# Splitting the feed-forward input inside the output projection, and multiplying by the row factor afterwards

## The chip, the cores and the metric

The kernel runs on one core of a Trainium2 chip. The metric is the device time of one execution in microseconds; the time of a kernel is the median of its runs. The engines are named as in the profile: PE (TensorE matmul), DVE (VectorE), ACT (ScalarE), POOL (GpSimd) and SP (SyncE, which issues the DMAs).

## What is computed

The reference is one inference step of a two-layer decoder trunk for a prompt of 1024 tokens and 8 sample tokens, 1032 rows in all, D_MODEL 1024, D_FF 3072. Each layer is a mixer and a convolved feed-forward block. What the change touches is the end of the mixer and the first half of the feed-forward:

```python
def _rmsnorm(x, g):
    r = lax.rsqrt(jnp.mean(x32 * x32, axis=-1, keepdims=True) + EPS)
    return (x32 * r * g).astype(x.dtype)

def _conv_ffn(x, buf, w_up, cw, cb, w_down):
    u = x @ w_up
    u, nbuf = _causal_dwconv(u, buf, cw, cb)      # three taps along the tokens
    return (jax.nn.gelu(u[..., :D_FF]) * u[..., D_FF:]) @ w_down, nbuf

# in _trunk, for each layer l
x = x + jnp.concatenate([main, mo], axis=-1) @ prm['w_out'][l]
hn = _rmsnorm(x, prm['norm_ffn_g'][l])
f, fc = _conv_ffn(hn, ffn_conv0[l], ...)
x = x + f
```

For the 8 samples the two earlier tokens of the convolution come from a state and not from the sequence. The factor r is one number for each token, the gain g one for each channel.

## The kernel before

**Layout.** Activations lie with the channels on the 128 partitions and the tokens along the row: 8 channel tiles of 1032 tokens. The tokens are cut into two halves of 516 (`HALF`) and four quarters of 258 (`QW`). A float32 operand is carried as a pair of reduced floats, hi (a rounded copy, made on ACT by `acopy`, L105) and lo (the operand less hi, made on DVE by `vtt`, L113, or on POOL by `gtt`, L116); each product is three matmuls (`mm3`, L298 to L300: hi by hi, hi by lo, lo by hi).

**Output projection** (`out_proj`, L775). For each half `hb` and each output tile `m`, two quarters of 24 matmuls of 258 columns, 48 matmuls a tile, 384 a half. `get` loads the weights one tile ahead and splits them (hi of 128x1024 on ACT, lo on POOL). The residual row of a tile comes by DMA when the tile is first met (`residual`, L768; in layer 0 from `x_t`, in layer 1 from a spill), DVE adds the finished sum to it, and `on_tile` (L1320) stores the new quarter to `rD` (L1322) and adds its square to a running sum over the tiles.

**Entry of the feed-forward** (`enter_ffn`, L1309). After the last tile of a half, `inverse` sums the squares over the channels with a matmul by ones (L1334) for both quarters and makes r of them; `norm` then scales every tile by g and r (DVE, L119) and makes the operands of the up projection. That projection is a seven-product scheme after Strassen and Winograd: per pair `j` of an up gate tile and an up value tile (24 pairs), products P1 to P7 of 4 x 3 matmuls on each half, 168 matmuls a pair. Its left operands are sums of quarters of the weights, made by `combine` (L832; 11 POOL operations of 128x512, of which 7 are lo parts, and 7 ACT copies a pair), its right operands B11, B21, B22, T1 to T4 sums of quarters of the normed residual, made by `norm`. The weights of pair 0 are made by `first_pair`, which is spawned when the first half of the projection is done; what is spawned advances a step at each `tick`.

**Up stage** (`ffn`, L858). The list `SEQUENCE` runs pair 0 one half at a time, then pairs 1 to 23 whole; weights are combined five products ahead (`AHEAD`). DVE adds the products from PSUM into two rows `ug` and `uv` of 1032. When a pair is done, `post` convolves: ACT makes the centre tap of 1032 columns and the bias (`act_conv`), DVE adds two shifted taps for each row (L119, 128x1023 and 128x1022) and the sample columns' state (128x8), ACT takes the gelu, DVE multiplies gate and value (128x1032), and SP stores the result to `gD`. POOL copies the last 10 columns of each row into `ul`.

**Order.** A scheduler places the instructions of DVE, POOL, PE and SP; ACT keeps the order of the program in layer 0 and in the feed-forward of both layers. Rows come from a pool of 44 buffers, small tiles from a pool of 12.

## Time and profile before

| | us |
|---|---|
| median of 3 runs | 2542.76 |
| range of the runs | 2539.66 to 2547.52 |
| the profiled execution | 2545.75 |
| its span | 2544.0 |
| PE busy in the span | 2339.4 (92%) |
| DVE, ACT, POOL busy | 1582.0, 1075.7, 1419.4 |
| mean granted TensorE clock | 0.961 |

The span is what the trace covers; 1.75 us of the profiled execution lie around it. A busy time is the sum of an engine's instructions. Granted clock 1.00 is 2.4 GHz and 0.50 is 1.2 GHz. In the timeline a number in brackets is the idle time ahead of an instruction and what ended it.

### The profile page before, as it was taken

How to read it: one execution, taken by the hardware profiler on the slowest of the kernel's cores; microseconds unless marked ns; L12 is line 12 of the kernel's file. 1: busy time of each engine (PE TensorE's matmuls, PEld its weight loads, DVE VectorE, ACT ScalarE, POOL GpSimd, SP SyncE). 2: the span in 40 equal slices, each digit the busy share in tenths (PEclk: the TensorE clock that was granted, in tenths of full speed). 3: DMA queues.
4: the chain of work that ended last, by engine and by line, in shares of the span. 5: the costliest groups of instructions: out<-in, count | busy, mean ns of one | idle time of the engine just before them, and what ended most of it. 6: DMA issues, size and time to landing. Idle time of an engine off the chain costs nothing.

```text
span 2544.0 us, 42855 instructions
## 1 busy us (share of the span) xinstructions
PE 2339.4 (92%) x16590; PEld 2255.1 (89%) x16590; DVE 1582.0 (62%) x2850; ACT 1075.7 (42%) x2253; POOL 1419.4 (56%) x1123
## 2 busy tenths in 40 slices
PE   7996877799999999999988988787999999999999
PEld 5896867789999999999977778687999999999999
DVE  6659975666666666432477789875666666663321
ACT  5665542344444344211265576643444344442110
POOL 2147743578888886312144356335888888853220
PEclk9998978899999999999999999898999999999999
DMA  4221124212222224421575544552122222254311
GB/s 165 85 69 56 44 77 150 75 67 76 76 84 85 83 76 177 164 91 58 166 237 171 201 141 133 149 166 73 67 84 84 84 76 76 76 211 135 97 56 64
DMA packets 142491, 273.64 MB, mean 108 GB/s; under 512 B 28544, under 2 KB 85456, under 8 KB 142288
## 3 DMA queue, kind: packets, MB, share of 16 engines
q1 hardware_dynamic: 142288, 270.91, 31.7%
q8 instruction: 130, 2.13, 0.3%
q14 instruction: 73, 0.60, 0.1%
HBM read 211.99 MB, written 58.87 MB: 106 GB/s over the span
## 4 chain that ended last, share of the span: by engine, by line
PE 64%; DVE 8%; issue 2%; ACT 2%; DMA 2%; POOL 1%; SPq 0%; POOLq 0%; ACTq 0%; DVEq 0%
PE ps L299 21%; PE ps L298 21%; PE ps L300 21%; DVE row L113 2%; ACT row L105 1%; DVE sm L113 1%; DVE row L119 1%; POOL row L116 1%; DVE ty L113 1%; DVE ty L396 1%; DMA row<-in_w_out 1%; DVE ty L119 0%; DMA row<-mD 0%; ACT sm L105 0%; PE ps L422 0%
## 5 line engine op out<-in xcount | busy, mean ns | idle before, releaser
L116 POOL TENSOR_TENSOR row<-row,row 128x512 fp32r<-128x512 f32 (+9 forms) x754 | 1164.6, 1566 | 789.4 <-ACT row L105 472.8
L298 PE MATMUL ps<-row,row 128*128 128x258 f32 (+4 forms) x5032 | 1511.9, 303 | 54.5 <-ACT row L105 44.4
L299 PE MATMUL ps<-row,row 128*128 128x258 f32 (+4 forms) x5032 | 1509.5, 302 | 27.9 <-DVE row L113 18.6
L300 PE MATMUL ps<-row,row 128*128 128x258 f32 (+4 forms) x5032 | 1471.0, 301 | 20.5 <-POOL row L116 20.5
L298 PEld LDWEIGHTS ps<-row,row 128*128 128x128 f32 x5032 | 963.7, 192 | 73.1 <-ACT row L105 49.8
L299 PEld LDWEIGHTS ps<-row,row 128*128 128x128 f32 x5032 | 965.1, 192 | 43.7 <-DVE row L113 24.1
L300 PEld LDWEIGHTS ps<-row,row 128*128 128x128 f32 x5032 | 948.4, 192 | 30.9 <-POOL row L116 23.4
L105 ACT ACTIVATE row<-row 128x512 fp32r<-128x512 f32 (+8 forms) x756 | 492.8, 690 | 922.5 <-POOL row L116 303.3
L113 DVE TENSOR_TENSOR row<-row,ps 128x258 f32<-128x258 f32 (+2 forms) x736 | 322.2, 444 | 700.7 <-PE ps L300 655.0
L119 DVE SCALAR_TENSOR_TENSOR row<-row,fw,row 128x1023 f32<-128x1023 f32 x192 | 264.7, 1397 | 67.3 <-ACT row L105 67.3
L113 DVE TENSOR_TENSOR row<-row,row 128x258 fp32r<-128x258 f32 (+7 forms) x268 | 242.9, 930 | 29.8 <-ACT row L105 15.8
L105 ACT ACTIVATE row<-ps 128x258 f32<-128x258 f32 (+6 forms) x430 | 157.3, 406 | 65.4 <-PE ps L300 26.1
L116 POOL TENSOR_TENSOR row<-row,ty 128x768 f32<-128x768 f32 (+2 forms) x56 | 77.3, 1381 | 157.7 <-DVE ty L413 55.2
L105 ACT ACTIVATE row<-row,fw 128x1032 f32<-128x1032 f32 x96 | 114.8, 1244 | 59.2 <-DVE row L113 59.1
L105 ACT ACTIVATE sm<-row 128x258 f32<-128x258 f32 (+3 forms) x130 | 54.6, 452 | 192.4 <-DVE row L113 129.4
L113 DVE TENSOR_TENSOR row<-row,sb 128x8 f32<-128x8 f32 x96 | 112.3, 1169 | 0.0
L113 DVE TENSOR_TENSOR sm<-sm,sm 128x258 f32<-128x258 f32 (+5 forms) x125 | 80.8, 652 | 24.8 <-ACT sm L105 23.3
L105 ACT ACTIVATE row<-ps,ty,ty 128x256 f32<-128x256 f32 (+1 forms) x160 | 87.4, 564 | 8.3 <-DVE ty L113 8.0
L105 ACT ACTIVATE sm<-ps 128x384 f32<-128x384 f32 (+5 forms) x156 | 65.0, 445 | 38.2 <-PE ps L431 24.1
L113 DVE TENSOR_TENSOR row<-ps,row 128x384 fp32r<-128x384 f32 (+2 forms) x125 | 63.3, 518 | 19.4 <-ACT row L105 8.1
L116 POOL TENSOR_TENSOR sm<-sm,row 128x192 f32<-128x192 f32 (+3 forms) x72 | 49.2, 696 | 34.1 <-ACT sm L105 18.6
L116 POOL TENSOR_TENSOR row<-row 128x512 f32<-128x512 f32 x48 | 62.0, 1291 | 2.5 <-DVE row L119 2.5
(164 smaller groups left out, 1485.5 us busy)
## 6 DMA issues: line engine op xcount, KB each, us to landing
row<-in_w_ffn_up SPq DMA_DIRECT2D x96, 512.0 KB, 3.2
gD<-row SPq DMA_DIRECT2D x48, 516.0 KB, 2.6
row<-gD SPq DMA_DIRECT2D x48, 516.0 KB, 6.2
row<-in_w_ffn_down SPq DMA_DIRECT2D x64, 384.0 KB, 3.0
row<-hD SPq DMA_DIRECT2D x48, 512.0 KB, 6.6
row<-in_w_out SPq DMA_DIRECT2D x32, 512.0 KB, 4.1
rD<-row SPq DMA_DIRECT2D x64, 129.0 KB, 2.0
row<-rD SPq DMA_DIRECT2D x16, 516.0 KB, 8.5
```

The source lines that it names most:

```text
L105: return nc.scalar.activation(out, in_, func, **kw)
L113: return V.tensor_tensor(out=out, in0=a, in1=b, op=op)
L116: return G.tensor_tensor(out=out, in0=a, in1=b, op=op)
L119: return V.scalar_tensor_tensor(out=out, in0=a, scalar=s, in1=b, op0=op0, op1=op1)
L298: T.matmul(out, ah, bh, start=first and j == 0, stop=False, skip_group_check=more)
L299: T.matmul(out, ah, bl, start=False, stop=False, skip_group_check=more)
L300: T.matmul(out, al, bh, start=False, stop=last and j == n - 1, skip_group_check=more)
L396: V.tensor_reduce(out=mx[:, c0 : c0 + m], in_=s3, axis=AX.X, op=amax, negate=True)
```

## The change

**1. The factor.** r is no longer multiplied into the operands. They are made of x times g alone, which is linear in them, and the finished rows `ug` and `uv` of every pair are multiplied by r (128x1032 on DVE, two a pair) ahead of the convolution. r itself is made once a layer, for the four quarters together, at step 10 of `SEQUENCE`; the multiplication by ones stands there, four matmuls.

**2. The split.** `on_tile` writes x times g back over the residual (ACT), and after each second-half tile `combine_x` makes T2, T3 and T4 of its four quarters (four differences and three lo parts of 128x258 on DVE, three hi on ACT). When a half is done `settle` makes the other four operands in copies of 516 columns (ACT), with lo on DVE for the gate half and POOL for the other. The tiles run in the order 0, 4, 1, 5, 2, 6, 3, 7.

**3. The residual.** It comes in half rows, two channel tiles in a row, and one fetch ahead of its use.

**4. The weights of pair 0.** `first_pair` is spawned ahead of the projection, one half earlier.

**5. The samples.** The state is added for 12 pairs at once on POOL, with gelu and gate over 96 columns (`samples`), and stored apart. The centre tap's gate side, gelu, gate multiplication and store are 1024 columns wide; the two 128x8 additions of a pair are gone.

```diff
+    def unspill(t, hb, kk):
+        for a in range(2):
+            k, d = kk + 4 * a, t[:, a * HALF : a * HALF + HALF]
+            if hb == 0:
+                SY.dma_start(d[:, : 4 * P].rearrange("p (i t) -> p i t", i=4), xD[0:4, :, k, :].rearrange("i p t -> p i t"))
+                SY.dma_start(d[:, 4 * P : HALF], xD[4, :, k, : HALF - 4 * P])
...
+    def residual(l, hb, kk):
+        t = row()
         if l:
-            return unspill(m)
-        t = row()
-        SY.dma_start(t[:, :NT], I["x_t"][:, m, :])
+            unspill(t, hb, kk)
+        else:
+            SY.dma_start(
+                t[:, : 2 * HALF].rearrange("p (a t) -> p a t", a=2),
+                I["x_t"].rearrange("p (a k) t -> p a k t", a=2)[:, :, kk, hb * HALF : hb * HALF + HALF],
+            )
         return t
...
+        fetch()
         for hb in range(2):
-            for m in range(KD):
+            for m in TILES:
                 key = f"out{l}.{hb}.{m}"
                 wh, wl = get(key, 1, 1)
-                if x[m] is None:
-                    x[m] = residual(l, m)
+                if m < 4:
+                    fetch()
...
-                    vtt(x[m][:, c0 : c0 + QW], x[m][:, c0 : c0 + QW], p[:, :QW], add)
-                    on_tile(q, m)
+                    on_tile(hb, part, m, p[:, :QW])
                     tick()
...
         def act_conv(u, t):
+            vtt(u[:, :NT], u[:, :NT], factor()[:, :NT], mul)
             a = row()
-            act(a[:, :NT], u[:, :NT], AF.Identity, scale=fwc(2, t), bias=fbc(t))
+            act(a[:, :SEQ], u[:, :SEQ], AF.Identity, scale=fwc(2, t), bias=fbc(t))
...
-            vtt(a[:, SEQ:NT], a[:, SEQ:NT], sb3[:, :, t], add)
...
-            vtt(ag[:, :NT], ag[:, :NT], av[:, :NT], mul)
-            SY.dma_start(gD[l, j], ag[:, :NT])
+            vtt(ag[:, :SEQ], ag[:, :SEQ], av[:, :SEQ], mul)
+            SY.dma_start(gD[l, j, :, :SEQ], ag[:, :SEQ])
+            if j % SG == SG - 1:
+                samples(j - SG + 1)
...
+        def samples(j0):
+            pair = []
+            for t0 in (j0, KF + j0):
+                t = sm()[:, : 8 * SG].rearrange("p (b j) -> p b j", b=8)
+                w = fw[:, None, 2 * MU + t0 : 2 * MU + t0 + SG].to_broadcast([P, 8, SG])
+                gtt(t, ul3[:, 2:10, t0 : t0 + SG], w, mul)
+                gtt(t, t, sb3[:, :, t0 : t0 + SG], add)
+                pair.append(t)
+            act(pair[0], pair[0], AF.Gelu_apprx_tanh)
+            o = sm()[:, : 8 * SG].rearrange("p (j b) -> p j b", b=8)
+            gtt(o.rearrange("p j b -> p b j"), pair[0], pair[1], mul)
+            SY.dma_start(gD[l, j0 : j0 + SG, :, SEQ:NT].rearrange("j p b -> p j b"), o)
...
+            if q == 10:
+                factor()
...
+        def on_tile(hf, part, m, p):
+            q = 2 * hf + part
+            xs, t = place(hf, part, m), sm()
+            vtt(t[:, :QW], xs, p, add)
+            SY.dma_start(rD[l, m, :, QB[q] : QB[q] + QW], t[:, :QW])
+            acopy(xs, t[:, :QW], scale=g_ffn[l][m])
...
+            if part == 0 and wait:
+                combine_x(*wait.pop())
+            if part == 1 and m >= 4:
+                wait.append((hf, m - 4))
+
+        def combine_x(hf, kk):
...
+            vtt(t3, d, b, sub)
+            vtt(b, b, a, sub)
+            vtt(t2, d, b, sub)
+            vtt(t4, c, t2, sub)
+            for name, t in (("T3", t3), ("T2", t2), ("T4", t4)):
...
+                split(name, kk, hf, own[name][:, o : o + QW], own[name][:, o + QW : o + HALF], t)
+
+        def settle(hf):
...
+                    acopy(hi, raw)
+                    (gtt if a else vtt)(lo, raw, f(hi), sub)
...
+        gen["w"] = spawn(first_pair())
+
         def on_half(hf):
...
-            gen[hf] = start(norm(hf))
-            if not hf:
-                gen["w"] = spawn(first_pair())
+            gen[hf] = start(settle(hf))
```

Three places of the order, before and with the change. First POOL in layer 0's projection, at the tiles of the first half; `in_w_out` rows are the projection's weights, 128x1024 their lo parts. Before:

```order
L116 TENSOR_TENSOR row_699_3862<-row_692_3797,row_698_3861 128x1024
L116 TENSOR_TENSOR row_707_3930<-row_700_3865,row_706_3929 128x1024
L116 TENSOR_TENSOR row_715_3998<-row_708_3933,row_714_3997 128x1024
L116 TENSOR_TENSOR row_731_4089<-row_716_4001,row_730_4088 128x1024
L116 TENSOR_TENSOR row_647_3464<-row_669_3595,row_646_3463 128x258
L116 TENSOR_TENSOR row_651_3472<-row_685_3731,row_650_3471 128x258
```
With the change (row_664 and row_665 hold the two raw weight tiles of pair 0):

```order
L118 TENSOR_TENSOR row_672_3601<-row_659_3489,row_671_3600 128x1024
L118 TENSOR_TENSOR row_681_3673<-row_665_3530 128x512
L118 TENSOR_TENSOR row_677_3638<-row_664_3528,row_677_3638 128x512
L118 TENSOR_TENSOR row_681_3673<-row_681_3673,row_664_3528 128x512
L118 TENSOR_TENSOR row_664_3528<-row_664_3528,row_665_3530 128x512
L118 TENSOR_TENSOR row_682_3676<-row_681_3673,row_682_3676 128x512
L118 TENSOR_TENSOR row_684_3680<-row_673_3604,row_683_3679 128x1024
L118 TENSOR_TENSOR row_681_3673<-row_664_3528,row_681_3673 128x512
L118 TENSOR_TENSOR row_696_3735<-row_664_3528,row_696_3735 128x512
L118 TENSOR_TENSOR row_700_3771<-row_664_3528,row_700_3771 128x512
L118 TENSOR_TENSOR row_702_3775<-row_685_3683,row_701_3774 128x1024
```
Before, POOL has nothing but the projection's lo parts up to the norm's 128x258 pieces; with the change, the weight sums and lo parts of pair 0 (128x512) stand between them, up to five between two lo parts.

Second, SP at the start of the same projection. Before:

```order
L251 DMA row_633_3326<-in_w_out 128x1024
L1286 DMA out_1<-yl_144 128x54
L251 DMA row_658_3487<-in_w_out 128x1024
L772 DMA row_659_3489<-in_x_t 128x1032
L802 DMA row_662_3524<-in_ffn_state 128x768
L1322 DMA rD_91<-row_659_3489 128x258
L805 DMA out_9<-row_662_3524 1024x1x48
L1322 DMA rD_91<-row_659_3489 128x258
L251 DMA row_668_3593<-in_w_out 128x1024
L772 DMA row_669_3595<-in_x_t 128x1032
```
With the change:

```order
L253 DMA row_633_3326<-in_w_out 128x1024
L783 DMA row_656_3483<-in_x_t 128x2x516
L1326 DMA out_1<-yl_144 128x54
L253 DMA row_659_3489<-in_w_out 128x1024
L783 DMA row_660_3491<-in_x_t 128x2x516
L844 DMA row_664_3528<-in_w_ffn_up 128x1024
L844 DMA row_665_3530<-in_w_ffn_up 128x1024
L823 DMA row_666_3532<-in_ffn_state 128x768
L1366 DMA rD_91<-sm_662_3518 128x258
L826 DMA out_9<-row_666_3532 1024x1x48
L1366 DMA rD_91<-sm_668_3588 128x258
```
The residual's DMA stands ahead of the store of `out_1` and is followed by the next one ahead of the first `rD` store; the two loads of pair 0's weights (`in_w_ffn_up`) have come in.

Third, DVE in one pair of the steady up stage, from the last additions of a pair to its gate multiplication; `ps` are products in PSUM, `fw` holds the taps, `sb` the sample state. Before:

```order
L113 TENSOR_TENSOR row_834_5100<-row_834_5100,ps_837_5124 128x258
L113 TENSOR_TENSOR row_838_5137<-row_838_5137,ps_845_5211 128x258
L113 TENSOR_TENSOR row_838_5137<-row_838_5137,ps_846_5224 128x258
L119 SCALAR_TENSOR_TENSOR row_849_5298<-row_838_5137,fw_100,row_849_5298 128x1023
L113 TENSOR_TENSOR row_849_5298<-row_849_5298,sb_101 128x8
L119 SCALAR_TENSOR_TENSOR row_850_5304<-row_834_5100,fw_100,row_850_5304 128x1023
L113 TENSOR_TENSOR row_850_5304<-row_850_5304,sb_101 128x8
L119 SCALAR_TENSOR_TENSOR row_849_5298<-row_838_5137,fw_100,row_849_5298 128x1022
L119 SCALAR_TENSOR_TENSOR row_850_5304<-row_834_5100,fw_100,row_850_5304 128x1022
L113 TENSOR_TENSOR row_858_5372<-row_854_5336,ps_856_5346 128x258
L113 TENSOR_TENSOR row_858_5372<-row_854_5336,ps_857_5359 128x258
L113 TENSOR_TENSOR row_849_5298<-row_849_5298,row_850_5304 128x1032
```
With the change (row_861 holds the factor of the four quarters):

```order
L115 TENSOR_TENSOR row_907_5359<-row_907_5359,ps_910_5381 128x258
L115 TENSOR_TENSOR row_911_5394<-row_911_5394,ps_918_5468 128x258
L115 TENSOR_TENSOR row_907_5359<-row_907_5359,row_861_4969 128x1032
L115 TENSOR_TENSOR row_911_5394<-row_911_5394,ps_919_5481 128x258
L115 TENSOR_TENSOR row_911_5394<-row_911_5394,row_861_4969 128x1032
L121 SCALAR_TENSOR_TENSOR row_922_5556<-row_911_5394,fw_100,row_922_5556 128x1023
L121 SCALAR_TENSOR_TENSOR row_923_5562<-row_907_5359,fw_100,row_923_5562 128x1023
L121 SCALAR_TENSOR_TENSOR row_922_5556<-row_911_5394,fw_100,row_922_5556 128x1022
L121 SCALAR_TENSOR_TENSOR row_923_5562<-row_907_5359,fw_100,row_923_5562 128x1022
L115 TENSOR_TENSOR row_931_5629<-row_927_5594,ps_929_5603 128x258
L115 TENSOR_TENSOR row_931_5629<-row_927_5594,ps_930_5616 128x258
L115 TENSOR_TENSOR row_922_5556<-row_922_5556,row_923_5562 128x1024
```
The two 128x8 additions are gone, and a 128x1032 multiplication by the factor stands behind the last addition of each row, the first of them ahead of an addition from PSUM; the gate multiplication is 1024 wide.

## Rows read from the trace of the kernel before

**Rows 1.** The page, part 1: busy time of each engine, share of the span, instructions

```profile
PE 2339.4 (92%) x16590; PEld 2255.1 (89%) x16590; DVE 1582.0 (62%) x2850; ACT 1075.7 (42%) x2253; POOL 1419.4 (56%) x1123
```

**Rows 2.** Windows of both up stages: stretch, PE, PEld, DVE, ACT, POOL busy, clock, DMA

```profile
550.00:950.00 400.00, 399.76 (x3335) 399.56 (x3334) 260.16 (x339) 168.24 (x280) 340.34 (x259) 1.00 0.23 80
1800.00:2200.00 400.00, 400.00 (x3327) 399.67 (x3326) 252.99 (x338) 168.22 (x280) 338.40 (x259) 1.00 0.23 80
```

**Rows 3.** Windows from output projection to second pair, layer 0, then layer 1

```profile
350.00:360.00 10.00, 2.73 (x11) 2.43 (x12) 3.79 (x7) 2.17 (x6) 1.87 (x3) 0.50 0.55 170
360.00:420.00 60.00, 47.81 (x359) 46.17 (x359) 19.71 (x39) 17.71 (x35) 24.00 (x14) 0.93 0.50 159
420.00:470.00 50.00, 32.50 (x204) 31.19 (x204) 41.97 (x68) 21.07 (x50) 31.63 (x26) 0.77 0.27 88
...
500.00:530.00 30.00, 21.62 (x128) 18.48 (x127) 23.18 (x52) 10.17 (x29) 14.05 (x17) 0.83 0.14 53
...
1680.00:1710.00 30.00, 25.53 (x189) 24.41 (x189) 25.17 (x51) 14.15 (x35) 8.86 (x10) 0.89 0.30 103
1710.00:1740.00 30.00, 16.80 (x109) 16.09 (x109) 17.00 (x37) 12.84 (x29) 24.34 (x18) 0.77 0.23 75
...
1760.00:1790.00 30.00, 20.73 (x123) 17.32 (x122) 26.98 (x61) 13.00 (x36) 10.15 (x13) 0.86 0.14 42
```

**Rows 4.** Waits, 340 to 560 us: engine, waited for, total, times, longest

```profile
POOL row L116 <- ACT row L105: 100.6, 28, 12.0
...
DVE row L113 <- DMA row<-in_x_t: 43.6, 8, 5.7
...
PE ps L1334 <- DVE sm L113: 6.6, 2, 5.6
```

**Rows 5.** Timeline, SP, layer 0 projection: start, duration, queue, line

```profile
351.60 0.38 SPq L772 DMA_DIRECT2D row<-in_x_t  x1
...
374.79 0.80 SPq L1322 DMA_DIRECT2D rD<-row  x2
...
382.19 0.80 SPq L1322 DMA_DIRECT2D rD<-row  x2
```

**Rows 6.** Timeline, POOL, same place; last column is idle time before and releaser

```profile
358.74 8.63 POOL L116 TENSOR_TENSOR row<-row,row 128x384 fp32r<-128x384 f32 x8 [8.13 <-ACT row L105]
...
376.57 2.39 POOL L116 TENSOR_TENSOR row<-row,row 128x1024 fp32r<-128x1024 f32 x1 [4.74 <-ACT row L105]
```

**Rows 7.** Timeline, DVE, same place

```profile
359.11 8.55 DVE L113 TENSOR_TENSOR row<-row,row 128x384 fp32r<-128x384 f32 x8 [0.33 <-ACT row L105]
...
375.24 0.77 DVE L113 TENSOR_TENSOR sm<-sm,sm 128x258 f32<-128x258 f32 x2 [0.15 <-ACT sm L105]
```

**Rows 8.** Timeline, POOL, one steady pair

```profile
711.24 7.30 POOL L116 TENSOR_TENSOR row<-row,row 128x512 f32<-128x512 f32 x5
...
718.63 2.29 POOL L116 TENSOR_TENSOR row<-row,row 128x512 fp32r<-128x512 f32 x1
723.90 3.64 POOL L116 TENSOR_TENSOR row<-row,row 128x512 fp32r<-128x512 f32 x2 [2.98 <-ACT row L105]
727.50 1.29 POOL L116 TENSOR_TENSOR row<-row 128x512 f32<-128x512 f32 x1
```

**Rows 9.** Timeline, DVE, the same pair

```profile
718.49 1.27 DVE L119 SCALAR_TENSOR_TENSOR row<-row,fw,row 128x1023 f32<-128x1023 f32 x1
719.68 1.26 DVE L113 TENSOR_TENSOR row<-row,sb 128x8 f32<-128x8 f32 x1
720.87 2.47 DVE L119 SCALAR_TENSOR_TENSOR row<-row,fw,row 128x1022 f32<-128x1022 f32 x2
723.25 0.75 DVE L113 TENSOR_TENSOR row<-row,ps 128x258 f32<-128x258 f32 x2
723.92 1.22 DVE L113 TENSOR_TENSOR row<-row,row 128x1032 f32<-128x1032 f32 x1
```

**Rows 10.** Groups by line and shape, 550 to 990 us: busy, mean ns, idle before

```profile
L867 POOL COPY ul<-row 128x10 f32<-128x10 f32 x44 | 8.9, 201 | 0.0
```

More of the change, by code (lines that the diff above doesn't have):

```diff
@@ L37 @@
 DCH = 6
+SG = 12
 NDC = KF // DCH
@@ L856, in up_weights, with ffn @@
         return load_pair, combine, made
-    def ffn(l, x, ops, need, weights, on_block, store=None):
+    def ffn(l, ops, need, factor, weights, on_block, store=None):
         ul3 = ul.rearrange("p (c t) -> p c t", c=10)
@@ L1309, in enter_ffn, with split @@
     def enter_ffn(l, x, mh, ml):
-        ops, gen, sums = {}, {}, {}
-        def split(name, kk, hf, pair, raw, on_pool):
-            hi, lo = pair
+        ops, gen, sums, own, wait = {}, {}, {}, {}, []
+        rf = []
+        def split(name, kk, hf, hi, lo, raw):
             acopy(hi, raw)
-            (gtt if on_pool else vtt)(lo, raw, f(hi), sub)
-            ops[name, kk, hf] = pair
-        def cols(q):
-            return slice(QB[q], QB[q] + QW)
-        def on_tile(q, m):
-            SY.dma_start(rD[l, m, :, cols(q)], x[m][:, cols(q)])
+            vtt(lo, raw, f(hi), sub)
+            ops[name, kk, hf] = hi, lo
@@ L1323, in on_tile, with place @@
+        def place(hf, part, k):
+            o = (k // 4) * HALF + part * QW
+            return x[hf, k % 4][:, o : o + QW]
+        def on_tile(hf, part, m, p):
[4 more added lines that the diff above has]
+            acopy(xs, t[:, :QW], scale=g_ffn[l][m])
             if m == 0:
                 sums[q] = sm()
[L1325 removed]
+                act(sums[q][:, :QW], t[:, :QW], AF.Square)
@@ L1326, in on_tile @@
             else:
-                t = sm()
-                act(t[:, :QW], x[m][:, cols(q)], AF.Square)
-                vtt(sums[q][:, :QW], sums[q][:, :QW], t[:, :QW], add)
-        def inverse(q):
-            a = sums.pop(q)
-            p = ps()
-            T.matmul(p[:, :QW], ones, a[:, :QW], start=True, stop=True)
-            m, out, t = sm()[:, :QW], sm()[:, :QW], sm()[:, :QW]
-            ts(V, m, p[:, :QW], 1.0 / D, EPS, mul, add)
-            act(out, m, AF.Ln)
-            act(out, out, AF.Exp, scale=-0.5)
-            stt(t, m, -0.5, out, mul, mul)
-            vtt(t, t, out, mul)
-            stt(out, t, 1.5, out, add, mul)
-            return out
@@ new lines, in on_tile @@
+                s = sm()
+                act(s[:, :QW], t[:, :QW], AF.Square)
+                vtt(sums[q][:, :QW], sums[q][:, :QW], s[:, :QW], add)
+            if part == 0 and wait:
[3 more added lines that the diff above has]
+        def combine_x(hf, kk):
+            a, b = place(hf, 0, kk), place(hf, 1, kk)
+            c, d = place(hf, 0, kk + 4), place(hf, 1, kk + 4)
+            t3, t2, t4 = (sm()[:, :QW] for _ in range(3))
+            vtt(t3, d, b, sub)
[3 more added lines that the diff above has]
+            for name, t in (("T3", t3), ("T2", t2), ("T4", t4)):
+                if kk % 2 == 0:
+                    own[name] = row(F32R)
+                o = (kk % 2) * HALF
+                split(name, kk, hf, own[name][:, o : o + QW], own[name][:, o + QW : o + HALF], t)
@@ new lines, in inverse @@
+        def inverse():
+            rf.append(row())
+            for q in range(4):
+                a = sums.pop(q)
+                p = ps()
+                T.matmul(p[:, :QW], ones, a[:, :QW], start=True, stop=True)
+                m, t = sm()[:, :QW], sm()[:, :QW]
+                out = rf[0][:, QB[q] : QB[q] + QW]
+                ts(V, m, p[:, :QW], 1.0 / D, EPS, mul, add)
+                act(out, m, AF.Ln)
+                act(out, out, AF.Exp, scale=-0.5)
+                stt(t, m, -0.5, out, mul, mul)
+                vtt(t, t, out, mul)
+                stt(out, t, 1.5, out, add, mul)
@@ L1416, in need, with factor @@
                 advance(gen[hf])
-        return on_tile, on_half, need, ops, weights
+        def factor():
+            if not rf:
+                inverse()
+            return rf[0]
+        return on_tile, on_half, need, ops, weights, factor
     def mgetA(k, c0, n):
```

108 lines of the change are left out of this document (40 added, 68 removed).

## The prediction

> **What bounds the kernel now.** I read the page first, then windows, then the waits and timelines of the stretches that lose time. PE is busy for 92% of the span [rows 1], so the question is where it is not. In the two up stages it never is idle: 400 us hold 400 us of PE work, 3335 and 3327 matmuls, one every 0.120 us, at clock 1.00 [rows 2]. A pair of 168 matmuls takes 20.15 us there. Nothing makes that faster but fewer matmuls, and the change keeps their number; but POOL is at 340 of the same 400 us [rows 2], and how far that is from a bound decides half of this case.
>
> PE loses time between the start of the output projection and the second pair. At 0.120 us a matmul, each stretch of [rows 3] is short by its length less its count times 0.120. Layer 0: 350 to 360 loses 8.7 us, 360 to 420 16.9, 420 to 470 25.5, 500 to 530 14.6. Layer 1: 1680 to 1710 loses 7.3, 1710 to 1740 16.9, 1760 to 1790 15.2. The clock column (0.50 to 0.93) shows that part of each is PE running at its lower level behind a wait. That is 66 and 39 us.
>
> Three causes are to be seen. In layer 0's first half the residual is asked for by SP behind the stores of the tile before: the `rD` stores follow each other by 7.4 us [rows 5] while a tile is 48 x 0.120 = 5.8 us of PE, and DVE waits 43.6 us in all for `x_t` [rows 4]. After a half PE waits for the sums that go into the multiplication by ones, 5.6 us the longer time [rows 4]. Then the norm and the split come in one block, in which POOL works on pieces of the norm and on pair 0's weights at the same time and waits 100.6 us for ACT [rows 4].
>
> **The change part by part.**
>
> *Entry, the gain.* With the split made tile by tile and no factor needed, the ones-matmul leaves both half boundaries: 5.6 us in 360 to 420, and the 7.3 us of 1680 to 1710. The block of norm and split behind the first half (25.5 and 16.9 us) shrinks to `settle`, four times two copies of 516 columns, beside 46 us of PE work; I leave 3 and 2 us. Behind the second half (14.6 and 15.2 us) pair 0's first half, 84 matmuls or 10 us, covers `settle`; I leave 3 us in each. The factor at step 10 has all its sums by then; its four ones-matmuls cost what they cost before. So far 5.6 + 22.5 + 11.6 = 39.7 us in layer 0 and 7.3 + 14.9 + 12.2 = 34.4 in layer 1.
>
> *Entry, what takes the place.* The first half of the projection now carries pair 0's weights. POOL has 8 lo parts of 128x1024 at 2.39 us [rows 6] and 11 operations of 128x512 at 1.25 (1.29 less the overlap of neighbours) [rows 8, 10]: 19.1 + 13.8 = 33 us. DVE has four differences and three lo parts for each of four `kk`, and 16 additions of squares, all with two inputs in SBUF, 44 at 0.38 (two take 0.77 [rows 7]): 17 us. If these exclude each other, as lo parts on both engines do in the mixer's rest (8 on POOL take 8.63 us, 8 on DVE 8.55, at the same time [rows 6, 7]), 50 us have to fit beside 46 us of PE. In layer 1 the half ran without a stall, so it lengthens, and I charge 6 us. In layer 0 the half was already longer by 17 us, and the residual now comes early (order of SP: ahead of the `out_1` store, the next one ahead of the `rD` store), up to 5 us earlier at the first tile. The slower half is then POOL's instead of SP's; I give 3 us. Layer 1's smaller residual DMAs (4 to 6 for each row, 47 SP instructions more in all) are issued one row ahead and lie under PE work.
> Sum at the entries: 42.7 + 28.4 = 71 us, between 53 (7 us more stay at each of the two big places and at layer 0's first half) and 86 (these stalls vanish and the 8.7 us of 350 to 360 too).
>
> *Steady pairs, the loss.* Each pair gets two multiplications of 128x1032 on DVE, nearest to the gate multiplication, 1.22 us [rows 9]. DVE is busy 260 of 400 us, and PE would not notice if only DVE counted. But POOL's row of one pair shows more. Its operations of 128x512 take 1.29 us alone and 2.29 at 718.63, when DVE began a tap at 718.49; two take 3.64 at 723.90, beside the gate multiplication at 723.92, and five take 7.30 [rows 8, 9]. The 128x8 addition at 719.68 takes 1.26 us and ends with POOL's 2.29 us operation at 720.92. Additions from PSUM stay at 0.42 beside POOL [rows 9]. So a DVE operation with two SBUF inputs and a POOL operation exclude each other, and each one that comes between costs POOL 1.00 to 1.10 us.
> By that sum a pair takes 11 x 1.25 + 2 x 0.15 (copies, 0.20 less overlap [rows 10]) = 14.05 us of POOL, three DVE operations that come between, 3.1, and an idle time of 2.98 in which the other two taps run [rows 8, 9]: 20.13, the pair's time. With the change seven DVE operations stand against POOL: 14.05 + 7 x 1.04 = 21.3 us if the idle time fills up, 1.2 more than PE needs. The dropped 128x8 additions give DVE time back, and POOL next to nothing, since their own work is a few hundredths.
> 22 pairs (0 and 1 are made at the entry) x 1.2 = 26 us. The bulk samples add 10 POOL operations of 128x96 a layer, between the copy's 0.20 and a 128x512's 1.29 [rows 8, 10], nearer the copy by their size: 3 us. 29 us a layer, 58 in both. The floor is nothing, if POOL has slack that I don't see; the ceiling stands under the rivals.
>
> The Trainium skill has this rule in "SBUF — State Buffer", section "SBUF: two separate sides": a DVE operation with two SBUF inputs and a GpSimd operation take a shared port pair as an exclusive lock for the whole instruction. The rows agree that one waits for the other; by the whole instruction (1.22 us and not 1.04) a pair would be 14.05 + 7 x 1.22 = 22.6 us and the loss 57 us a layer. The rows' own stretch is the smaller one and makes the sum; the other is a rival below.
>
> *Net.* -71 + 58 = -13 us on the profiled 2545.75, or 2533; the median lies 3 us below that execution, so 2530.
>
> **The rivals.**
> *The exclusion costs more: slower.* POOL's idle 2.98 us stays, since ACT keeps program order: its hi copies, on which POOL waits, stand behind the gelu, which stands behind four taps that now start two multiplications later. Then a pair is 14.05 + 5 x 1.03 + 2.98 = 22.2 us, the loss (2.05 x 22 + 3) x 2 = 96, and the time 2530 + 38 = 2568. It decides from 21.8 us a pair, where (1.6 x 22 + 3) x 2 = 77 is over the gain. For it: the waits of ACT and POOL on each other; against it: POOL's idle time is there because it is ahead of PE, and a POOL that is behind does not wait for PE's results.
> *Each operation shuts POOL out for its whole time.* At the gate multiplication's 1.22 [rows 9] for each of the seven a pair takes 14.05 + 8.5 = 22.6 us, the loss is 2 x (2.45 x 22 + 3) = 114 and the time 2586. The lengthened POOL rows speak against it: 1.00 to 1.10 for each.
> *The exclusion costs little: much faster.* POOL finds room in the idle time, PE stays full, 20.15 us a pair; only the samples cost. Loss 6, net -65, 2478. For it: no PE wait is in 400 us now; against it: the sum of 20.13 has no room.
> *The entry gains little.* The change moves the jam of POOL into the first half but doesn't end it: the projection's lo parts wait behind up to five weight operations (order of POOL), each such wait lets the clock fall as in 420 to 470 (0.77), and the entries give 30 in place of 71. With the same loss: 2571.
>
> **How the numbers follow.** A measurement tells about 0.3%, 7.6 us. The forecast, 2530, has a chance of 0.48 and its own range from 2500 to 2555 (entries 53 to 86, loss 45 to 70). The dear exclusion 0.20, the whole-time one 0.05, the cheap one 0.20, the entry without gain 0.07. The range takes in most of the dear and of the cheap case: 2476 to 2578. Faster by over 0.3%: 0.29 of the forecast's 0.48, 0.20 of the cheap, and 0.02 of the dear, 0.51. Within 0.3%: 0.12 of the forecast, 0.03 of the dear, 0.02 of the entry, 0.17. Slower: the rest, 0.07 + 0.15 + 0.05 + 0.05 = 0.32.
>
> **What would show it.** In the profile after: windows of 400 us in the up stage with fewer than 3335 matmuls (about 3150 at 21.3 us a pair, 3020 at 22.2), PE waiting there for POOL rows, POOL's operations at 2.3 us more often and its idle time for ACT gone (if it is still about 3 us, the first rival holds). At the entries: no ones-matmul after a half, over 380 matmuls in the 50 us behind the first half, pair 1 of layer 0 about 43 us nearer to the start of the projection and of layer 1 about 28, and a first half that ends late for POOL. The forecast is wrong if PE keeps 0.120 us a matmul in the up stage, or if the first half of the projection takes over 60 us.

## The result, and the profile after

The changed kernel takes 2571.61 us (median of 4 runs, 2565.08 to 2572.15), the kernel before 2543.23 beside it: a ratio of 1.0104, 95% interval 1.0086 to 1.0121. By the medians it is slower by 28.4 us, where 13 us faster was forecast.

The page's busy times of the changed kernel, to be held against [rows 1]:

```profile
PE 2351.4 (91%) x16590; PEld 2258.6 (88%) x16590; DVE 1694.0 (66%) x2796; ACT 1097.1 (43%) x2289; POOL 1528.5 (59%) x1103
```

PE has as many matmuls and nearly the same busy time. DVE has 54 instructions fewer and 112 us more, POOL 20 fewer and 109 us more: instructions of both became longer. Where that tells is seen in the windows of the two up stages, which answer [rows 2] (stretch, PE, PEld, DVE, ACT and POOL busy with their counts, clock, DMA share, GB/s):

```profile
550.00:950.00 400.00, 382.20 (x3099) 376.02 (x3098) 277.81 (x315) 153.16 (x259) 364.73 (x245) 0.99 0.22 75
1800.00:2200.00 400.00, 382.17 (x3118) 375.76 (x3117) 283.52 (x318) 154.61 (x261) 369.00 (x247) 1.00 0.22 76
```

3099 and 3118 matmuls in place of 3335 and 3327, at a clock of 0.99 and 1.00 as against 1.00: PE now waits there. The exact measure of a pair is the store of its result by SP. In the timeline of `gD` stores a row gives the count, their durations in ns, and the start of the first and the last; here pairs 0 to 22 of layer 0 and then of layer 1, first of the kernel before, then of the changed one:

```profile
L888 SPq DMA_DIRECT2D gD<-row x23: 320/326/327, 543.9 to 987.0; - x23
L888 SPq DMA_DIRECT2D gD<-row x23: 319/327/327, 1810.9 to 2253.2; - x23
```

```profile
L910 SPq DMA_DIRECT2D gD<-row x23: 319/327/327, 508.7 to 986.9; - x23
...
L910 SPq DMA_DIRECT2D gD<-row x23: 320/326/327, 1802.8 to 2278.7; - x23
```

These four rows hold most of the balance, of the two profiled executions (spans of 2544.0 and 2570.1 us). Pair 0 of layer 0 is done 35.2 us earlier; 3.2 of them lie ahead of the projection's first `rD` store (357.8 us before, 354.6 now). The 22 pairs behind it take 478.2 us in place of 443.1, so 35.1 us are lost again, and at pair 22 both kernels stand at 987. In layer 1 the pairs take 475.9 in place of 442.3, another 33.6 lost. Layer 1's projection begins later, by its first `rD` store, before and now:

```profile
L1322 SPq DMA_DIRECT2D rD<-row x32: 319/320/530, 1635.6 to 1760.5; - x32
```

```profile
L1366 SPq DMA_DIRECT2D rD<-sm x32: 319/320/1085, 1639.5 to 1760.8; - x32
```

From there to pair 0's store it is 163.3 us in place of 175.3. With 0.6 in the rest:

| stretch | forecast, us | measured, us |
|---|---|---|
| entry of layer 0 | -42.7 | -35.2 |
| 22 pairs, layer 0 | +29 | +35.1 |
| from there to layer 1's projection | 0 | +4.0 |
| entry of layer 1 | -28.4 | -12.0 |
| 22 pairs, layer 1 | +29 | +33.6 |
| rest | 0 | +0.6 |
| sum | -13 | +26.1 |

The windows that answer [rows 3] show the same of the entries:

```profile
360.00:420.00 60.00, 51.38 (x389) 49.64 (x387) 46.16 (x70) 31.81 (x68) 39.45 (x25) 0.94 0.46 134
420.00:470.00 50.00, 48.17 (x385) 47.76 (x386) 33.78 (x63) 27.27 (x58) 21.27 (x12) 0.97 0.46 152
470.00:500.00 30.00, 24.43 (x173) 23.39 (x172) 18.09 (x32) 12.89 (x24) 14.67 (x12) 0.89 0.10 36
...
1680.00:1710.00 30.00, 17.44 (x144) 17.03 (x142) 24.44 (x37) 17.00 (x36) 17.52 (x12) 0.84 0.58 172
```

Behind layer 0's first half 385 matmuls stand in 50 us where 204 stood. But 470 to 500 has only 173, and 1680 to 1710 has 144 where 189 stood before (the stages are shifted by a few us between the two kernels): the entries have new holes.

Pair by pair the stores show two kinds. Of the 44 pairs 30 take 21.1 to 21.3 us and 11 take 22.4 to 22.7; the two in which POOL makes the bulk samples take 26.3 and 23.9, and the one ahead of the first of these 20.1. Two pairs show what the engines do (start, duration, line, idle time ahead and its releaser in brackets). First POOL and then DVE in a usual one:

```profile
795.74 10.98 POOL L118 TENSOR_TENSOR row<-row,row 128x512 fp32r<-128x512 f32 x7
806.65 2.39 POOL L890 COPY ul<-row 128x10 f32<-128x10 f32 x2
809.00 2.34 POOL L118 TENSOR_TENSOR row<-row,row 128x512 fp32r<-128x512 f32 x1
811.93 3.86 POOL L118 TENSOR_TENSOR row<-row,row 128x512 fp32r<-128x512 f32 x2 [0.60 <-ACT row L107]
```

```profile
800.83 1.23 DVE L115 TENSOR_TENSOR row<-row,row 128x1032 f32<-128x1032 f32 x1
801.97 0.41 DVE L115 TENSOR_TENSOR row<-row,ps 128x258 f32<-128x258 f32 x1
802.49 1.80 DVE L115 TENSOR_TENSOR row<-row,row 128x1032 f32<-128x1032 f32 x1
805.61 6.80 DVE L121 SCALAR_TENSOR_TENSOR row<-row,fw,row 128x1023 f32<-128x1023 f32 x4 [1.32 <-ACT row L107]
```

Then the same at one of the 11, two pairs on:

```profile
839.55 9.66 POOL L118 TENSOR_TENSOR row<-row,row 128x512 f32<-128x512 f32 x6
849.15 0.33 POOL L890 COPY ul<-row 128x10 f32<-128x10 f32 x2
851.05 1.94 POOL L118 TENSOR_TENSOR row<-row,row 128x512 fp32r<-128x512 f32 x1 [1.57 <-ACT row L107]
855.82 3.65 POOL L118 TENSOR_TENSOR row<-row,row 128x512 fp32r<-128x512 f32 x2 [2.84 <-ACT row L107]
```

```profile
843.41 2.38 DVE L115 TENSOR_TENSOR row<-row,row 128x1032 f32<-128x1032 f32 x1
845.71 0.41 DVE L115 TENSOR_TENSOR row<-row,ps 128x258 f32<-128x258 f32 x1
846.23 1.82 DVE L115 TENSOR_TENSOR row<-row,row 128x1032 f32<-128x1032 f32 x1
849.36 5.91 DVE L121 SCALAR_TENSOR_TENSOR row<-row,fw,row 128x1023 f32<-128x1023 f32 x4 [1.31 <-ACT row L107]
```

In [rows 9] an operation like the multiplications by the factor took 1.22 us. The first of them takes 1.23 us in the usual pair and 2.38 in the other, with POOL at work beside both; the second takes 1.80 and 1.82. The addition from PSUM between them keeps its 0.41. Where the first one is late, so is ACT's convolution, and POOL waits twice for ACT, 4.4 us in all and not 0.6.

### The profile page after: what moved, and what is told of

Read it like the earlier page. It is cut to its first block, busy times and chain, and to the rows that moved or that the text cites. A ratio compares the mean times of both kernels' runs of the same rounds, so it can differ in the third digit from the quotient of the medians.

```text
span 2570.1 us, 42946 instructions
## 1 busy us (share of the span) xinstructions
PE 2351.4 (91%) x16590; PEld 2258.6 (88%) x16590; DVE 1694.0 (66%) x2796; ACT 1097.1 (43%) x2289; POOL 1528.5 (59%) x1103
## 4 chain that ended last, share of the span: by engine, by line
PE 51%; DVE 18%; POOL 8%; ACT 5%; issue 4%; DMA 2%; SPq 0%; DVEq 0%; ACTq 0%; POOLq 0%
PE ps L302 16%; PE ps L300 16%; PE ps L301 16%; DVE row L115 9%; POOL row L118 6%; ACT row L107 5%; DVE row L121 4%; DVE sm L115 2%; POOL ul L890 1%; DVE ty L115 1%; DVE ty L398 1%; DMA row<-in_cache_mem_k 0%; ACT sm L107 0%; POOL sm L118 0%; PE ps L424 0%
## 5 line engine op out<-in xcount | busy, mean ns | idle before, releaser
L118 POOL TENSOR_TENSOR row<-row,row 128x512 fp32r<-128x512 f32 (+9 forms) x714 | 1186.3, 1682 | 698.9 <-ACT row L107 396.4
L107 ACT ACTIVATE row<-row 128x512 fp32r<-128x512 f32 (+9 forms) x684 | 473.7, 728 | 799.5 <-POOL row L118 311.6
L115 DVE TENSOR_TENSOR row<-row,ps 128x258 f32<-128x258 f32 (+2 forms) x672 | 295.4, 446 | 569.7 <-PE ps L302 561.5
L115 DVE TENSOR_TENSOR row<-row,row 128x1032 f32<-128x1032 f32 (+7 forms) x292 | 390.9, 1352 | 37.5 <-ACT row L107 23.8
L121 DVE SCALAR_TENSOR_TENSOR row<-row,fw,row 128x1023 f32<-128x1023 f32 x192 | 313.0, 1688 | 67.1 <-ACT row L107 67.1
L107 ACT ACTIVATE row<-row,fw 128x1024 f32<-128x1024 f32 x96 | 114.1, 1236 | 194.6 <-DVE row L115 194.6
L890 POOL COPY ul<-row 128x10 f32<-128x10 f32 x96 | 84.1, 905 | 8.7 <-DVE row L115 8.7
L107 ACT ACTIVATE row<-sm,pack 128x258 f32<-128x258 f32 x64 | 32.4, 507 | 68.7 <-DVE sm L115 61.4
```

The source lines that it names most:

```text
L107: return nc.scalar.activation(out, in_, func, **kw)
L115: return V.tensor_tensor(out=out, in0=a, in1=b, op=op)
L118: return G.tensor_tensor(out=out, in0=a, in1=b, op=op)
L121: return V.scalar_tensor_tensor(out=out, in0=a, scalar=s, in1=b, op0=op0, op1=op1)
L890: G.tensor_copy(out=ul3[:, :, t], in_=u[:, SEQ - 2 : NT])
```

## The experiments

All times are medians beside the kernel before on the same chip (2540.5 to 2543.4). A pair is the mean over 22 pairs, layer 0 and layer 1, from the `gD` stores.

### Is it the multiplications? (e1)

```diff
-            vtt(u[:, :NT], u[:, :NT], factor()[:, :NT], mul)
```

> The changed kernel without the two multiplications by the row factor in each pair (the up rows stay without the factor, nothing else is left out). Theory A, exclusion: the two DVE operations with two SBUF inputs cost POOL, and through it PE, the 1.4 us that a pair has grown by (21.5 us with the sample pairs left out, 20.15 before). Without them a pair takes 20.15 to 20.4 us, 400 us of the up stage hold over 3280 matmuls, and the time is 2571.6 - 2 x 22 x 1.3 = about 2514 (2505 to 2525). Theory B, the pair grew by something else in the change (bulk samples, ACT's order, the narrower rows): the pair stays over 21 us and the time over 2555.

2493.08 us (ratio 0.9806, 0.9781 to 0.9831), a pair 20.19 and 20.10 us. Theory A holds against B: without them nothing else of the change lengthens the mean pair by more than 0.05 us. The time is 12 us below the expected range: 68 of the 78.5 us gained are in the pairs, 8.5 between pair 22 of layer 0 and layer 1's projection, a stretch whose spread is told with e12. The rest of the change is worth 49.7 us in this run. The window of the up stage:

```profile
550.00:950.00 400.00, 400.00 (x3332) 399.89 (x3332) 230.22 (x297) 168.89 (x281) 340.55 (x263) 1.00 0.23 77
```

### That they run, or that ACT waits for them? (e2)

```diff
+        spare = []
...
-            vtt(u[:, :NT], u[:, :NT], factor()[:, :NT], mul)
+            if not spare:
+                spare.append(row())
+            vtt(spare[0][:, :NT], u[:, :NT], factor()[:, :NT], mul)
```

> The changed kernel with the two multiplications of a pair written into a spare row that nobody reads (so the up rows stay without the factor): the same two operations on DVE, but ACT's convolution does not wait for them. Theory A, exclusion: what costs is that they run at all; a pair stays at 21.2 to 21.7 us and the time at 2562 to 2576. Theory C, the chain: what costs is that ACT, in program order, waits for the multiplied rows with the weights' hi copies behind it; then a pair falls to 20.2 to 20.5 us and the time to 2510 to 2525.

2582.92 us, a pair 22.12 and 22.09. Nobody waits for the products and the kernel is slower than with them in the chain, by 11 us, more than theory A's upper end. Theory C falls as the whole cause. In its timeline the second multiplication stands between two taps of the convolution, for which the gelu waits, and behind the gelu the hi copies; most pairs take 22.0 us, with POOL idle for 2.8 us in each.

### The same arithmetic, read from PSUM (e3)

```diff
...
+                    u, c = {"P4": (uv, a), "P5": (uv, b), "P3": (ug, b)}[name]
+                    if j:
+                        o = bank[j, "X", hf][:, :QW] if name == "P5" else p
+                        vtt(o, u[:, c], p, add)
+                        vtt(u[:, c], o, factor()[:, c], mul)
...
```

For P2 the ACT copy from PSUM becomes a multiplication by the factor; pair 0 keeps the long multiplications.

> The changed kernel with the factor applied from PSUM in pairs 1 to 23: the last addition of each quarter writes its sum into PSUM, and eight multiplications of 128x258 read it there, so each has one SBUF input and one in PSUM (two of them take the place of ACT copies). DVE gets some 0.5 us a pair more work than by the two long multiplications. Theory A, exclusion between two-SBUF-input operations and POOL: a pair takes 20.15 to 20.5 us, the time is 2510 to 2525. Theory C, the chain, or DVE's sheer work: a pair stays at 21 us or more, the time at 2555 or more.

2504.78 us (0.985, 0.9833 to 0.9866), 5 us below the expected range, a pair 20.31 and 20.30, within it: theory A. The window has DVE busier than in the changed kernel (299.79 of 400 us, there 277.81) and PE full:

```profile
550.00:950.00 400.00, 398.82 (x3317) 398.42 (x3316) 299.79 (x454) 154.57 (x238) 328.41 (x263) 1.00 0.23 78
```

So it is not DVE's work that cost but the form of the operation; its place in ACT's chain changes too, but taking it out of the chain alone gained nothing (e2). POOL's sums of weights show it. Groups of the same 400 us by shape (count, busy, mean ns), first of the changed kernel, then of this one:

```profile
L118 POOL TENSOR_TENSOR row<-row,row 128x512 fp32r<-128x512 f32 x129 | 233.7, 1829 | 31.1 <-ACT row L107 31.1
...
L890 POOL COPY ul<-row 128x10 f32<-128x10 f32 x36 | 32.9, 945 | 3.2 <-DVE row L115 3.2
```

```profile
L118 POOL TENSOR_TENSOR row<-row,row 128x512 fp32r<-128x512 f32 x138 | 209.6, 1544 | 66.5 <-ACT row L107 66.5
...
L891 POOL COPY ul<-row 128x10 f32<-128x10 f32 x40 | 16.2, 405 | 0.0
```

The lo parts fall from 1829 to 1544 ns and the copies of 10 columns from 945 to 405, and POOL waits longer for ACT, 66.5 us: it is ahead again.

### One multiplication (e7) and two on the kernel before (e8)

```diff
-            vtt(u[:, :NT], u[:, :NT], factor()[:, :NT], mul)
+            if t < KF:
+                vtt(u[:, :NT], u[:, :NT], factor()[:, :NT], mul)
```

> The changed kernel with the factor on the gate row alone (the value row stays without it): one long multiplication a pair. If POOL's time and the exclusions add up to a bound, as in the prediction's sum, a pair takes 14.05 + 6 x 1.04 = 20.3 us, next to the 20.2 without any, and the time is 2495 to 2508: the first of the two is nearly free and the second costs all. If each multiplication delays PE by the same, a pair takes 20.8 to 20.95 and the time is 2525 to 2538.

2544.02 us, a pair 21.18 and 21.06. Both guesses miss: 20.3 was the sum's, 20.8 to 20.95 the even share's. The first multiplication costs 0.97 us a pair (21.12 less 20.15), the second 0.57 (21.69 less 21.12). POOL still waits 51.0 us for ACT in 400 us here, 2.83 us in most pairs, and with that time left in, the form of the prediction's first rival gives what most pairs take (21.0): 14.05 + 4 x 1.03 + 2.83 = 21.0.

```diff
+        spare = []
...
+            if not spare:
+                spare.append(row())
+            vtt(spare[0][:, :NT], u[:, :NT], u[:, :NT], mul)
             a = row()
             act(a[:, :NT], u[:, :NT], AF.Identity, scale=fwc(2, t), bias=fbc(t))
```

> The kernel before with two multiplications of 128x1032 from SBUF added to each pair, written to a spare row that nobody reads, and nothing else changed: the disputed cost by itself, at the old entry. Theory A, exclusion: a pair grows from 20.14 to between 21.3 (the prediction's sum) and 22.1 us (what the changed kernel took with its multiplications aside), the time to between 2593 and 2630. Rival: the kernel before has room for them (POOL waits 2.98 us a pair for ACT), a pair stays under 20.4 us and the time under 2555.

2623.5 us (1.0316, 1.0292 to 1.034), a pair 22.03 and 22.05, at the upper end of theory A. The old entry is untouched, so 80.9 us are the price of two such operations a pair by themselves. POOL's groups in the up stage:

```profile
L116 POOL TENSOR_TENSOR row<-row,row 128x512 fp32r<-128x512 f32 x128 | 220.3, 1739 | 51.2 <-ACT row L105 51.2
L116 POOL TENSOR_TENSOR row<-row,row 128x512 f32<-128x512 f32 x55 | 89.3, 1624 | 0.0
```

### The samples (e9)

```diff
+            vtt(a[:, SEQ:NT], a[:, SEQ:NT], sb3[:, :, t], add)
...
-            if j % SG == SG - 1:
-                samples(j - SG + 1)
```

> The changed kernel with the samples convolved pair by pair as in the kernel before (two 128x8 additions on DVE a pair, rows of 1032 columns for the centre tap, gelu, gate and store). The trace of the changed kernel puts 5.0 and 2.6 us beyond a usual pair at the two bulk places within the up stages and a store 2.5 us after the last pair's at their ends. Theory G, the bulk samples stop ACT, in program order, while POOL makes them: these 8 to 12 us are saved, and the additions, held up by POOL but shorter than a lock-out of their own, cost under 5: 2560 to 2568. Rival H: two more operations with two SBUF inputs in each pair shut POOL out as the multiplications do, about 0.1 to 0.4 us a pair: 2570 to 2585.

2581.5 us, 10 us over the changed kernel; a pair 22.08 and 22.07. The time and the pairs are rival H's, but not its reason: POOL's busy time in 400 us falls, from 364.73 to 346.73. What grows is its wait for ACT, 53.9 of 400 us, 2.9 us in nearly every pair, as long as before the change (2.98 [rows 8]) and as in e2 (53.5) and e8 (51.2). Theory G falls too: in the changed kernel ACT waits only 0.28 us for the samples (at 743.20).

### POOL's idle time (e10)

```diff
-AHEAD = 5
+AHEAD = 6
```

> The changed kernel with the weights combined six products ahead instead of five, so that in ACT's order each hi copy stands one product earlier against the convolution and the gelu. If the part of a pair that exclusion alone does not explain is POOL's idle time behind ACT's order (1.7 us a pair in the changed kernel, 2.8 with the multiplications aside), it shrinks and a pair goes from 21.5 to 20.9 to 21.3 us, the time to 2545 to 2563. Rival: the hi copies then wait for POOL's sums or for rows (44 buffers) at the new place, and a pair stays at 21.5 us or grows: 2565 or more.

2550.54 us (21 under the changed kernel), a pair 21.55 and 21.35, in the expected range of times, and a little above that of the pair. Of the 21 us 10 are in the pairs. POOL's wait for ACT is gone:

```profile
L118 POOL TENSOR_TENSOR row<-row,row 128x512 fp32r<-128x512 f32 x132 | 242.8, 1865 | 1.2 <-ACT row L107 1.2
```

The windows of the two layers:

```profile
550.00:950.00 400.00, 381.10 (x3129) 376.76 (x3129) 292.37 (x317) 155.60 (x259) 385.60 (x248) 1.00 0.21 74
1800.00:2200.00 400.00, 389.15 (x3153) 381.99 (x3152) 285.11 (x319) 158.78 (x266) 397.21 (x251) 1.00 0.24 76
```

POOL is busy for 385.60 and 397.21 of 400 us, so here it is the bound by itself, at 21.35 us a pair in the layer where it is full. Without the idle time a pair is what the sum of the prediction said (21.3); with POOL's 2.8 to 3.0 us left in it, it is what its first rival said (22.2; measured 22.03 to 22.12 in e2, e8, e9). The changed kernel has two kinds of pairs: most keep 0.6 or 0.7 us of idle time and take what the sum said, and about one in four has the 4.4 us of the rows above. The mean is 1.7 us (31.1 us in 18.5 pairs).

### Layer 1's entry (e4)

```diff
+        if l:
+            mget(6, QW, QW)
         fetch()
...
+                if l and hb == 0 and m == 2:
+                    mget(6, 3 * QW, QW)
```

> The changed kernel, with layer 1's mixer rows of the second and third token block fetched and split earlier: the second block's ahead of the first residual rows, the third block's within the first half of the projection. Theory D, SP's order: PE's waits of 8.6 us in the first tile and 13.5 us at the start of the second half of layer 1's projection come from those loads standing behind the residual's small DMAs and the rD stores; they fall to under 4 and under 1 us and the time to about 2555 (2550 to 2562). Theory E, POOL's jam: the first half ends when POOL has made pair 0's weights, so PE waits elsewhere instead and the time stays within 5 us of 2571.6.

2558.76 us, 12.8 under the changed kernel. From the first `rD` store to pair 0's store it is 148.1 us in place of 163.3: 27.2 under the kernel before, where 28.4 was forecast. The whole time gains less than these 15.2 us, since layer 1's pairs took 3.5 us more in this run. Theory D holds in the main; no wait of PE in the first tile is over 2 us (8.6 in the changed kernel, 3.4 before), but that at the second half is 4.6 us and not under 1. The rows of SP and PE, first of the changed kernel:

```profile
1704.48 0.49 SPq L567 DMA_DIRECT2D row<-xD  x1
1705.08 4.27 SPq L1852 DMA_DIRECT2D row<-mD  x8
```

```profile
1711.21 0.80 PE L300 MATMUL ps<-row,row 128*128 128x258 f32 x2 [13.53 <-ACT row L107]
```

and of e4:

```profile
1670.43 1.90 SPq L1856 DMA_DIRECT2D row<-mD  x4
```

```profile
1707.04 0.58 PE L300 MATMUL ps<-row,row 128*128 128x258 f32 x1 [4.62 <-ACT row L107]
```

In the kernel before the same eight loads were issued from 1674.49 to 1680.7, ahead of the last tiles of the first half:

```profile
1674.49 1.44 SPq L1819 DMA_DIRECT2D row<-mD  x3
1676.75 0.33 SPq L1322 DMA_DIRECT2D rD<-row  x1
1677.13 3.61 SPq L1819 DMA_DIRECT2D row<-mD  x5
```

With the change they stood behind the residual's rows for the second half, at the place where PE already needed them.

### Together, and pair 0's weights (e5, e6, e11)

e5 has the edits of e3 and e4.

> The changed kernel with both edits that gained alone: the factor applied from PSUM (2504.8) and layer 1's mixer rows fetched earlier (2558.8, 12.8 us under the changed kernel). If the two losses are apart, one in the pairs and one in the entry of layer 1, the gains add: 2504.8 - 12.8 = 2492 (2487 to 2497). If the earlier fetch gained only because POOL or DVE was late in that kernel's entry, less than half of it is left: 2498 or more.

2493.43 us (0.9806, 0.9788 to 0.9823): the gains add nearly in full, 11.4 of 12.8 us. e6 puts the weights of pair 0 back into the second half:

```diff
-        gen["w"] = spawn(first_pair())
...
             gen[hf] = start(settle(hf))
+            if not hf:
+                gen["w"] = spawn(first_pair())
```

> The same, with the weights of pair 0 made in the second half of the projection, as in the kernel before. Theory E, POOL's jam in the first half: PE's waits for POOL there, 1.75, 2.07, 1.06, 0.73 us and others in layer 0 and the slower clock behind them, go, and the second half, in which POOL was busy 15 of 50 us, takes the 14 us of weights: 6 to 12 us under the kernel without this edit. Rival F: the weights of pair 0 come late for pair 0's first products, PE waits for POOL there and the jam has only moved: within 3 us of that kernel, or above it.

2491.85 us, within the spread of e5: rival F. Layer 0's first half ends 6 us sooner (its sixteenth `rD` store 52.0 us after the first, in e5 57.9) and its second half takes 7 us more (55.5, in e5 48.4). The jam has moved. In layer 1 the first half takes 53.6 us in e5 and 48.3 in e6 between its first and its last `rD` store, so the weights cost it 5 us, near the 6 that were charged; even so it is no longer than before the change (55.3).

> The fastest kernel so far (factor from PSUM, mixer rows earlier, weights of pair 0 in the second half; 2491.9) with six products ahead. Pairs take 20.3 us there and PE's floor is 20.15, so at most 2 x 23 x 0.15 = 7 us are to be had: 2485 to 2492. Rival: the one row more that is held costs at the entries or at the end of the stage: 2494 or more.

2495.01 us, its interval (0.9808 to 0.9841 of before) above that of e6 (0.9784 to 0.9814) for the most part: with POOL ahead, one product more gains nothing, as the rival said.

### The factor's place (e12)

In the changed kernel's trace ACT's table load for the factor stands at 481.62, and its hi copy for pair 1 comes after the eight operations that follow. POOL and PE there:

```profile
489.69 2.88 POOL L118 TENSOR_TENSOR row<-row,row 128x512 fp32r<-128x512 f32 x2 [13.09 <-ACT row L107]
```

```profile
489.66 0.58 PE L300 MATMUL ps<-row,row 128*128 128x258 f32 x1 [3.41 <-ACT row L107]
```

POOL has stood still for 13.1 us, and PE has waited 3.4. e12 is e6 with the factor made earlier:

```diff
-            if q == 10:
+            if q == 4:
                 factor()
```

> The fastest kernel so far (factor from PSUM, mixer rows earlier, weights of pair 0 in the second half; 2491.9) with the factor made at step 4 of the sequence, not at step 10. In the changed kernel's trace ACT holds eight operations and a table load for the factor from 481.6 to 488.6 us, the first hi copy of pair 1 comes at 489.0, POOL has waited 13.1 us for it and PE then 3.4, with 1.3 and 1.9 more behind it. If that is what the factor costs in its place, the hi copy comes some 6 us earlier and 3 to 6 us are saved in layer 0, 1 to 3 in layer 1: 2483 to 2488. If the factor then holds up the split of the second half's operands instead (PE waits at steps 7 to 10), the time stays within 2 us of 2492 or rises.

2478.87 us (0.9751, 0.9736 to 0.9766), 13 us under e6 where 4 to 9 were expected. 7.3 us of it are at the two entries by the stores (first `rD` to pair 0: 153.0 and 139.6 us, in e6 155.6 and 144.3). POOL's idle time at that place in layer 0 goes from 13.2 us in e6 to 9.0, so most of it is not the factor's; PE still waits 3.0 and 2.9 us in this entry. Another 6 us lie ahead of layer 0's projection and between the layers, where the two kernels have the same code. These two stretches differ as much between other runs: in e8, which has the old code there, the first `rD` store of layer 0 comes 3.6 us earlier than in the kernel before, and from pair 22 of layer 0 to layer 1's projection the fourteen profiles take 644 to 654 us. So 7.3 us are what the edit is shown to give.

This is the fastest version: 2.5% under the kernel before and 3.6% under the changed one.

## Why the prediction was wrong, step by step

The forecast is off by 39 us: 16.4 in the entry of layer 1, 10.7 in the pairs, 7.5 in the entry of layer 0, 4.6 in the rest. Two rivals named 2568 and 2571 us, but neither describes the kernel: they have 71 and 30 us at the entries and lose 96 and 58 in the pairs, and measured were 47 and 69. That their times are near is luck.

**The exclusion in the pairs: right in kind, too small.** e1, e3 and e8 show it each in its way: without the two operations a pair is 20.15, with an input in PSUM 20.3, and on the untouched old kernel they cost 1.9 us a pair. The step that failed is "21.3 us if the idle time fills up". It does in 30 of 44 pairs, which take 21.1 to 21.3 us; in 11 it does not, and each of these is 1.2 us longer, 13 us in all. The first rival's reason, that ACT keeps program order and POOL's hi copies stand behind convolution and gelu, is real: e10 moved the copies one place and POOL's wait for them went from 31.1 us to 1.2 in 400. The argument against that rival, that a POOL that is behind doesn't wait, was wrong: POOL's wait hangs on ACT and DVE, and DVE can be late too, beside POOL (2.38 us for a multiplication of 1.22). Why it is late in just these pairs was not followed up. With the samples the loss was 35.1 and 33.6 us in place of 29 each.

**The length of a lock-out.** The rival of 22.6 us by the whole duration did not occur without idle time: e10 gives 21.35, and (21.35 - 14.05) / 7 is 1.04 us for each operation, as the rows of before had it. With the idle time left in e8 agrees: (22.06 - 2.84 - 14.05) / 5 is 1.03. The Trainium skill, "SBUF — State Buffer", section "SBUF: two separate sides", names the DVE operation with two SBUF inputs as the one that shuts GpSimd out. The trace agrees (e3: with one of the inputs in PSUM a pair falls from 21.7 to 20.3 us); for the price of each, the stretch measured here is the number to take.

**The dropped 128x8 additions: not next to nothing.** The prediction said that dropping them gives POOL "next to nothing". e9 puts them back, and POOL's idle time with them: 0.35 us a pair more in layer 0 and 0.44 in layer 1, 17 us in the pairs although the bulk work goes. They cost POOL no busy time (it falls). That they delay the gelu, and with it the hi copies, is likely, since one of the two takes 1.25 us between the taps in e9; but e9 also widens ACT's operations and the gate, and the two were not separated.

**The bulk samples: too cheap.** 3 us of POOL were charged for a layer, ten operations "nearer the copy by their size". The five of the first bulk take 3.7 us by themselves, the two that read `ul` 1.3 us each, as long as one of 128x512, and PE waits for POOL behind the first four:

```profile
740.19 2.63 POOL L118 TENSOR_TENSOR sm<-ul,fw 128x96 f32<-128x96 f32 x2
742.78 0.72 POOL L118 TENSOR_TENSOR sm<-sm,sb 128x96 f32<-128x96 f32 x2
...
746.91 0.39 POOL L118 TENSOR_TENSOR sm<-sm,sm 128x96 f32<-128x96 f32 x1
```

```profile
745.77 0.58 PE L302 MATMUL ps<-row,row 128*128 128x258 f32 x1 [3.77 <-POOL row L118]
```

The pair at the bulk takes 26.3 us in layer 0 and 23.9 in layer 1; together with the pair ahead of it that is 3.9 and 2.6 over two usual ones. In e3, where POOL is ahead, it is 1.0 and 0.7: most of the cost belonged to POOL being late.

**The entry of layer 0: right in kind, 7.5 us too large.** The hole behind the first half is gone (385 of 417 possible matmuls in 420 to 470) and no multiplication by ones stands behind a half. The step that failed is the factor at step 10, of which only PE's share was counted ("its four ones-matmuls cost what they cost before"). ACT's eight operations and a table load stand, in program order, ahead of pair 1's hi copies; moved to step 4, they give 2.6 us back in layer 0 and 4.7 in layer 1 (e12). What else is in layer 0's 7.5 us was not found.

**The entry of layer 1: 16.4 us too large.** That layer 1's smaller residual DMAs "are issued one row ahead and lie under PE work" was the failed step. They do, but SP's order was read for layer 0 alone. The mixer's rows, which no part of the diff names, slid behind them, and PE waited 8.6 (before 3.4) and 13.5 us. With them fetched early, the second block's earlier than in the kernel before, the entry gains 27.2 (e4), 1.2 under the forecast. That it comes so near is in part luck: the first half is not longer than before (54.5 us in e4, 55.3), where 6 us were charged, and the factor's place costs 4.7 that were not. The late start (4.0 us between the layers) lies within the spread of that stretch over the runs, 644 to 654 us; 3.2 of it stand in pair 23, with the second bulk (26.0 us after pair 22, before the change 22.8, in e9 without bulk 22.7).

**The rival of the first half's jam** was not the cause: moving pair 0's weights changes nothing that can be told (e6 against e5).

**A reading and the bounds.** The row that is cited for additions from PSUM "beside POOL" (723.25 [rows 9]) falls into POOL's idle time, 720.92 to 723.90 [rows 8]; the addition at 845.71 above, while POOL is busy from 839.55 to 849.2, shows the same 0.41. The entries' bounds do not follow from their terms: three times 7 us off 71 leave 50 and not 53, and with the 11 us of stalls and the 8.7 us added it is 91 and not 86.

## What to carry to other kernels

Where POOL is near its bound, count DVE's operations by form, not by busy time: each one with two inputs in SBUF costs POOL about a microsecond at this size, however short DVE's own list is, and reading one input from PSUM takes it off the count. A step moved to where its inputs are ready can be paid on the engine that keeps program order (here ACT with the factor, 7.3 us), so look at what stands behind it there. After a change that adds DMAs to a queue, read the order of that queue in every stage, for the loads that the diff does not name.

## What was not expected of the hardware

The first operation that was added cost more (0.97 us a pair) than the second (0.57). POOL's wait for ACT fits that: it is 51.0 us in 400 with one and 31.1 with both, so the second takes up a part of it. And an operation for which nobody waits (e2) cost more than the same one in the chain, 22.1 us a pair against 21.7: POOL's wait for ACT stayed at 53.5 us in 400 there. A POOL copy of 10 columns, 0.20 us alone, took 0.95 us in the mean in the changed kernel.
